# Two terms of a hand-written planner: how VectorE is shared with a cached-attention lane, and when TensorE takes a side step

## The chip, the cores and the metric

One Trainium2 chip, one NeuronCore. The metric is the device time of one launch in microseconds, as the median of several runs; for the kernel before it is 2890.09 us over three runs (2888.13 to 2892.71). The traces are of one further, profiled execution.

## The reference

Two decoder layers are computed for a prompt of 1,024 tokens and for 8 samples of 4 new tokens each, 1,056 rows of width 1,024 in all, with one set of weights, in float32. What matters here, in short:

```python
# layer 0: three dilated window attentions per head slot, mixed by their softmax weights
for g, (w, r) in enumerate(((128, 1), (512, 4), (2048, 16))):
    q, k = rope(rmsnorm(q)), rope(rmsnorm(k))
    prompt: o, lse = banded_attention(q, k, v)          # 128-wide bands, dilation r
    sample: s[b,t,h,j] = q . k_all[lb + t - r*j]        # j = 0..128, from the cache and the new rows
            o = softmax(s) @ v_all;  window buffers are shifted and returned
mix = sum_g softmax(lse)_g * o_g
# layer 1: S5 state space with GLU
# both layers: cross attention into 256 memory tokens, output projection, gated FFN with a width-3 convolution
```

`dilated_sample`, the sample's attention over its cached keys and values, is the part that the change names "the sample's cached attention". The rest of the two layers is the prompt's and the samples' projections, attentions, state space and FFN.

## The kernel before, in words

**Dense work.** Every projection runs on TensorE with activations and weights split in a high and a low part (three matmuls per product, `mm3`), in three column groups of 352 rows, into the four `pd` banks of PSUM. Weights come over the SyncE queue, ScalarE casts the high half (`whigh`) and VectorE subtracts the low half (`wlow`).

**Lanes.** All other work is written as Python generators, which sit in 14 queues, `self.lanes` (line 262 on). A generator issues some instructions and then yields what its next step needs: `yield x` means that the next step is TensorE's and reads tile `x`; `yield DVE, x` (or `ACT`, `POOL`) that it is another engine's; `yield WAIT` that it cannot go on yet. TensorE's steps of lanes are called side steps here; they write the four `pm` banks, and `pd` banks as well where the program only waits.

**The planner.** `Meter` (line 105 on) keeps a reckoned clock for every engine and a reckoned end for every written range. `note` (line 164) adds each instruction's cost by a formula: a matmul n/2400 + 0.0025 us, a VectorE operation 0.065 + 1.04 ns an element, 0.065 more with a scalar operand. `ready` (line 133) says when a step's inputs are there, with 0.2 us for another engine's result (0.06 for TensorE's own, 0.12 for VectorE's). These clocks only decide the order in which instructions are written down; on the chip each engine runs its own stream, and semaphores hold it where data is missing.

**The pump.** After every `mm3` of a dense product the kernel calls `pump` (line 329). It sets `now` to TensorE's reckoned clock + 0.1 us and calls `wtick` (line 390), which writes the casts and low halves of the next weights if ScalarE's or VectorE's clock is not past `now`. Then it goes through the lanes, by when their next step is due, lane 2 last, and takes up to four steps of each while `gate` (line 314) lies not past `now`; after one side step it leaves that lane. `gate` is the later of `due` (line 326, the inputs) and of the engine's clock, or for a side step of a free bank. Lane 2 is let through 0.6 us early. In `until` (line 360) the program writes no dense work; it sets `idle` and pumps until a condition holds, and a pump that moved nothing takes the step with the earliest gate.

**Lane 2** holds two kinds of generator. In layer 0 it is `swa` (line 1317), the samples' cached attention, one for each of 4 heads x 3 groups: on VectorE alone, it multiplies keys of the cache with the query (`tensor_tensor_reduce`, `M<-L,L` in the rows, and a read of the accumulator) and then adds scaled values (`scalar_tensor_tensor`, `L<-L,T,L`), with a `yield DVE` after each fifth product. Its first step needs the query, new key and value that `swa_prep` (line 1282, lane 1) has sent through DRAM (`scr`) with DMAs on GpSimd's queue; the cache comes in chunks over SyncE's queue. In layer 1 lane 2 holds `s5_out` (line 1821), whose steps are TensorE's.

**Around it.** `run` (line 2449) goes through the 12 pairs of head and group. Each turn begins with an `until` that lets at most 1, 2, 3 and 1 generators stand in lanes 0 to 3, then writes three dense projections (and on some turns one of the cross attention's queries) and appends `attn` (line 1079, lane 0), whose `scores` (line 1138) go to lanes 3 and 13, `swa_prep` and `swa`. The cross attention's `cross_p` (line 911) and `cross_s` (line 952) and the mixing of the groups, `combine_head` (line 1198), run in other lanes. After the last turn come `mem_kv(1)`, an `until` for the first mixed half and `swa_final(0)` (line 1405), the output projection `out_half` (line 1918), an `until` for the second half, and `finish` (line 746). In layer 1 the S5 chain is `s5_states` (line 1783, lane 0), `s5_out` (lane 2), `glu_in` and `s5_final`; `glu` (line 1896) begins with an `until` on them; `cross_gather` (line 1926) fetches the cross attention's result for the second `out_half`.

The step that ends a group of five products, and the lane's early pass, read:

```python
                if pi % 5 == 4:
                    yield DVE
...
            for _ in range(4):
                if not len(lane) or self.gate(lane) > now + 0.6 * (lane is self.lanes[2]):
                    break
```

All instructions are recorded through one helper, so the rows give line 216 (L216) throughout; they are told apart by tiles: `pd` dense, `pm` side steps, `L` the cached attention's ring, queries and sums (and other large tiles), `M`, `S` and `T` small work tiles, `A` and `B` large ones.

Of the kernel before, what the change touches and what calls it, by code (L numbers as in the profile page):

```python
# [248 lines left out]
class Kernel:  # L249
# [64 lines left out]
    def gate(self, lane):  # L314

        if lane.has(WAIT):
            return math.inf
        if lane.side():
            first = self.m.t[lane.gate[0]]
        else:  # L320
            first = self.m.bank_free("m", PM) if self.m.taken("m") < PM - 1 else math.inf
            if self.idle and self.m.taken("d") < PD - 1:
                first = min(first, self.m.bank_free("d", PD))
        return max(first, self.due(lane))

    def due(self, lane):
        return self.m.ready(lane.gate[lane.side():], lane.gate[0] if lane.side() else "tensor") if not lane.has(WAIT) else math.inf
# [1 line left out]
    def pump(self, force=False):  # L329
        now, moved = self.m.t["tensor"] + 0.1, False  # L330
        self.wtick(now)
        for lane in sorted((x for x in self.lanes if len(x)), key=lambda x: (x is self.lanes[2], self.due(x))):
            if len(lane) and lane.has(WAIT):
                lane.step()
                moved |= not lane.has(WAIT)
            for _ in range(4):
                if not len(lane) or self.gate(lane) > now + 0.6 * (lane is self.lanes[2]):
                    break
                side = lane.side()
                lane.step()  # L340
                moved = True
                if not side:
                    break
        if force and not moved:
            lanes = [x for x in self.lanes if len(x)]
            if lanes:
                min(lanes, key=lambda x: (self.gate(x), x in self.lanes[0:3:2], self.due(x))).step()
        if self.bulk and self.bulk_on and now > self.bulk_at:
            self.bulk_at = now + 24.0
            o, i = self.bulk.popleft()  # L350
            self.nc.sync.dma_start(out=o, in_=i)
# [1890 lines left out]
    def up_out(self, ht, ua, ub):  # L2242

        a, b = self.B(), self.B()
        yield from self.conv_sb(ht, ua, a)
        tail = self.conv_sb(NHT + ht, ub, b)
        next(tail)
        yield
        next(tail)
        gate = self.hidden(ht, a, b)  # L2250
        next(gate)
        yield
        for _ in tail:
            pass
        self.convs = ht + 1
        yield
        yield from gate
# [363 lines left out]
```

## Time and profile before

| | |
|---|---|
| median of three runs | 2890.09 us (2888.13 to 2892.71) |
| the profiled execution | 2884.84 us |
| its span, first to last instruction | 2883.1 us |
| mean granted TensorE clock | 0.976 |
| VectorE busy | 2047.9 us (71%) |
| ScalarE busy | 1216.7 us (42%) |
| GpSimd busy | 517.6 us (18%) |

A row of a timeline reads: start and length in microseconds, engine, line, operation, tile written <- tiles read, shapes, count, and in brackets how long the engine had been idle before and what released it. PE is TensorE's matmuls, PEld its weight loads, DVE VectorE, ACT ScalarE, POOL GpSimd. PEclk is the TensorE clock that was granted, as a share of full speed (2.4 GHz at 1.0, 1.2 GHz at 0.5).

### The profile page before, as it was taken

Reading aid. Unit: us, or ns where it says so; the run is one execution under the profiler, and the core shown is the slowest. Engines: PE = TensorE matmul, PEld = TensorE weight load, DVE = VectorE, ACT = ScalarE, POOL = GpSimd, SP = SyncE. Lnnn points to the kernel's source line nnn. Section 1 sums busy time; section 2 is a strip of 40 time slices with the busy share of each in tenths; the row PEclk is TensorE's granted clock in tenths of the full one; section 3 lists DMA queues with packets and bytes.
Section 4 is the critical chain, followed back from the end, with each engine's and each line's share of the span. In section 5 each row is a group of like instructions: output and inputs, shape, how many; then the busy total and the mean of one; then the engine's idle time right before and its main releaser. Section 6 shows DMA issues by size and latency. Waiting matters only on the chain. (4 is left out here: it accounts for less than half of the span.)

```text
span 2883.1 us, 50916 instructions
## 1 busy us (share of the span) xinstructions
PE 2713.7 (94%) x18896; PEld 2601.1 (90%) x18896; DVE 2047.9 (71%) x5918; ACT 1216.7 (42%) x3045; POOL 517.6 (18%) x773
## 2 busy tenths in 40 slices
PE   7999888899979999999999998988999999999999
PEld 5999877899969999999999898877999999999998
DVE  7466876788885787878859776645477877876444
ACT  6555545455541544444432124346254444443111
POOL 2111222313222500000102555310241000000000
PEclk8999999999989999999999999999999999999999
DMA  7235567667673423333464435943443333346421
GB/s 251 85 93 146 174 185 218 197 178 198 186 202 129 155 92 115 125 119 122 156 224 140 157 118 158 269 116 113 159 141 125 125 118 104 118 133 244 150 79 68
DMA packets 357315, 431.56 MB, mean 150 GB/s; under 512 B 30502, under 2 KB 310196, under 8 KB 355644
## 3 DMA queue, kind: packets, MB, share of 16 engines
q1 hardware_dynamic: 328604, 359.77, 39.3%
q0 software_dynamic: 28464, 68.55, 7.9%
q8 instruction: 149, 2.44, 0.4%
q14 instruction: 98, 0.80, 0.1%
HBM read 345.10 MB, written 172.37 MB: 179 GB/s over the span
## 5 line engine op out<-in xcount | busy, mean ns | idle before, releaser
L216 PE MATMUL pd<-A,B 128*128 128x352 f32 (+2 forms) x10992 | 1784.6, 316 | 48.8 <-DVE B L216 32.3
L216 PEld LDWEIGHTS pd<-A,B 128*128 128x128 f32 x10992 | 1641.1, 190 | 76.7 <-issue 37.3
L216 DVE TENSOR_TENSOR B<-B,B 128x512 fp32r<-128x512 f32 (+7 forms) x604 | 511.9, 856 | 220.5 <-ACT B L216 215.3
L216 ACT CAST B<-B 128x512 fp32r<-128x512 f32 (+4 forms) x430 | 313.9, 751 | 660.0 <-DVE B L216 337.3
L216 PE MATMUL pd<-L,B 128*128 128x264 f32 (+1 forms) x2976 | 445.5, 302 | 2.3 <-DVE B L216 1.8
L216 PEld LDWEIGHTS pd<-L,B 128*128 128x128 f32 x2976 | 415.8, 189 | 5.6 <-DVE B L216 2.7
L216 DVE TENSOR_TENSOR B<-pd,B 128x352 f32<-128x352 f32 x408 | 202.2, 518 | 191.0 <-PE pd L216 189.0
L216 ACT COPY B<-pm 128x512 f32<-128x512 f32 (+5 forms) x261 | 130.8, 509 | 198.3 <-PE pm L216 189.8
L216 PE MATMUL pd<-B,B 128*128 128x264 f32 (+2 forms) x1306 | 204.6, 306 | 7.2 <-DVE B L216 7.2
L216 DVE SCALAR_TENSOR_TENSOR B<-B,S,B 128x1023 f32<-128x1023 f32 (+1 forms) x152 | 194.1, 1277 | 0.0
L216 PEld LDWEIGHTS pd<-B,B 128*128 128x128 f32 x1306 | 181.8, 190 | 11.2 <-ACT L L216 7.1
L216 PE MATMUL pm<-const,B 128*128 128x128 f32 (+6 forms) x1119 | 159.8, 272 | 25.1 <-DMA B<-in_g_mix 7.5
L216 PEld LDWEIGHTS pm<-const,B 128*128 128x128 f32 (+4 forms) x1119 | 129.7, 147 | 44.7 <-issue 20.9
L216 ACT COPY S<-pm 128x256 f32<-128x256 f32 (+5 forms) x277 | 87.5, 348 | 160.0 <-PE pm L216 132.3
L216 ACT COPY B<-pd 128x352 f32<-128x352 f32 (+4 forms) x211 | 105.4, 542 | 101.8 <-PE pd L216 96.7
L216 ACT CAST A<-B 128x352 fp32r<-128x352 f32 (+3 forms) x148 | 97.0, 668 | 109.7 <-DVE B L216 45.5
L216 ACT ACTIVATE B<-B 128x352 f32<-128x352 f32 (+3 forms) x127 | 94.2, 750 | 50.7 <-DVE B L216 45.5
L216 DVE SCALAR_TENSOR_TENSOR L<-L,T,L 128x128 f32<-128x128 f32 x404 | 110.6, 349 | 0.9 <-DMA L<-in_cache_win_kv 0.9
L216 DVE CUSTOM_DVE_ANT_0 M<-L,L 128x128 f32<-128x128 f32 x384 | 88.6, 290 | 27.1 <-DMA L<-scr 12.9
L216 POOL DMA_DIRECT2D out_s_conv<-B x12 | 6.2, 513 | 553.3 <-ACT B L216 553.3
L216 PE MATMUL pm<-const,S 128*128 128x128 f32 (+3 forms) x464 | 80.6, 281 | 24.2 <-ACT S L216 16.7
L216 ACT ACTIVATE B<-B,S 128x1056 f32<-128x1056 f32 x76 | 96.7, 1273 | 2.3 <-DVE B L216 2.3
(230 smaller groups left out, 2669.8 us busy)
## 6 DMA issues: line engine op xcount, KB each, us to landing
B<-in_w_up SPq DMA_DIRECT2D x88, 512.0 KB, 5.1
hd<-B SPq DMA_DIRECT2D x44, 528.0 KB, 3.0
B<-hd SPq DMA_DIRECT2D x44, 528.0 KB, 4.1
B<-in_w_down SPq DMA_DIRECT2D x44, 512.0 KB, 3.6
B<-in_w_in_a SPq DMA_DIRECT2D x40, 512.0 KB, 5.0
B<-xsp SPq DMA_DIRECT2D x32, 528.0 KB, 6.6
L<-in_cache_win_kv SPq DMA_DIRECT2D x16, 1024.0 KB, 8.6
L<-in_cache_win_kv SPq DMA_DIRECT2D x64, 256.0 KB, 5.9
```

The lines of the kernel that those rows point to most:

```text
L216: return f(*args, **kw)
```

## The change

The gate of a side step is put 0.8 us after its inputs are reckoned to be there, except while the program waits in `until`. In the pump, lane 2 gives up to one step instead of four, and it is no longer let through 0.6 us early; what holds for lane 2 holds for both kinds of generator in it.

```diff
--- before.py
+++ after.py
@@ -321,7 +321,7 @@
             first = self.m.bank_free("m", PM) if self.m.taken("m") < PM - 1 else math.inf
             if self.idle and self.m.taken("d") < PD - 1:
                 first = min(first, self.m.bank_free("d", PD))
-        return max(first, self.due(lane))
+        return max(first, self.due(lane) + (0.0 if self.idle or lane.side() else 0.8))
 
     def due(self, lane):
         return self.m.ready(lane.gate[lane.side():], lane.gate[0] if lane.side() else "tensor") if not lane.has(WAIT) else math.inf
@@ -333,8 +333,8 @@
             if len(lane) and lane.has(WAIT):
                 lane.step()
                 moved |= not lane.has(WAIT)
-            for _ in range(4):
-                if not len(lane) or self.gate(lane) > now + 0.6 * (lane is self.lanes[2]):
+            for _ in range(1 if lane is self.lanes[2] else 4):
+                if not len(lane) or self.gate(lane) > now:
                     break
                 side = lane.side()
                 lane.step()
```

## Rows read from the trace of the kernel before

**Rows 1.** The page, part 1: TensorE's busy time, share of the span, instructions.

```profile
PE 2713.7 (94%) x18896; PEld 2601.1 (90%) x18896; DVE 2047.9 (71%) x5918; ACT 1216.7 (42%) x3045; POOL 517.6 (18%) x773
```

**Rows 2.** Windows by stage; columns: us, busy PE, PEld, DVE, ACT, POOL, PEclk, DMA, GB/s.

```profile
80.00:290.00 210.00, 204.72 (x1355) 197.92 (x1355) 126.45 (x610) 112.91 (x371) 27.15 (x47) 0.99 0.36 107
290.00:580.00 290.00, 253.95 (x1780) 234.30 (x1779) 214.12 (x1089) 147.46 (x470) 82.22 (x127) 0.96 0.64 193
580.00:780.00 200.00, 194.91 (x1297) 189.49 (x1296) 169.60 (x874) 113.14 (x376) 49.72 (x78) 0.99 0.64 180
780.00:900.00 120.00, 102.08 (x574) 91.97 (x573) 96.29 (x363) 44.64 (x116) 27.58 (x35) 0.91 0.71 211
```

**Rows 3.** TensorE's waits, 290 to 580 us; columns: total us, times, longest.

```profile
PE pm L216 <- ACT B L216: 18.3, 6, 7.8
PE pm L216 <- ACT S L216: 12.9, 10, 3.4
```

**Rows 4.** VectorE's timeline from 523.5 us; columns: start, length, what, [idle before <-releaser].

```profile
524.33 0.86 DVE L216 TENSOR_SCALAR L<-L,T 128x128 f32<-128x128 f32 x4
525.11 4.28 DVE L216 SCALAR_TENSOR_TENSOR L<-L,T,L 128x128 f32<-128x128 f32 x16
529.31 0.15 DVE L216 TENSOR_TENSOR T<-B 128x4 f32<-128x4 f32 x1
```

**Rows 5.** TensorE's timeline, 523 to 533 us.

```profile
530.65 1.11 PE L216 MATMUL pm<-const,B 128*128 128x128 f32 x4 [4.77 <-ACT B L216]
```

**Rows 6.** TensorE's timeline, 318 to 326 us.

```profile
321.68 0.71 PE L216 MATMUL pm<-const,S 128*128 128x128 f32 x2 [3.44 <-ACT S L216]
...
325.58 0.86 PE L216 MATMUL pm<-const,S 128*128 128x128 f32 x2 [2.70 <-ACT S L216]
```

**Rows 7.** VectorE's timeline at 377 us.

```profile
377.26 1.78 DVE L216 CUSTOM_DVE_ANT_0 M<-L,L 128x128 f32<-128x128 f32 x1 [6.93 <-POOL B L216]
```

**Rows 8.** TensorE's timeline, 375 to 386 us.

```profile
383.84 1.08 PE L216 MATMUL pm<-B,M 128*32 128x256 f32 x8 [7.83 <-ACT B L216]
```

**Rows 9.** VectorE's groups by shape, 290 to 580 us; columns: count, busy, mean, idle before.

```profile
L216 DVE CUSTOM_DVE_ANT_0 M<-L,L 128x128 f32<-128x128 f32 x160 | 39.6, 296 | 20.8 <-POOL B L216 6.9 <-DMA L<-scr 6.6 <-DMA xo<-M 6.0
...
L216 DVE DVE_READ_ACCUMULATOR2_ANT T<- 128x1 f32 x192 | 15.6, 81 | 0.0
```

**Rows 10.** Windows after one wait and in the second layer; columns as in rows 2.

```profile
528.04:534.87 6.83, 4.22 (x17) 4.09 (x18) 6.38 (x23) 4.10 (x14) 3.13 (x3) 0.50 1.11 347
1908.90:1945.60 36.70, 24.70 (x160) 18.25 (x160) 24.63 (x92) 21.76 (x57) 4.64 (x7) 0.81 0.37 123
1945.60:2040.40 94.80, 86.51 (x669) 74.73 (x668) 48.70 (x142) 54.98 (x155) 11.51 (x18) 1.00 0.40 125
```

**Rows 11.** Timeline of all engines, 815 to 832 us.

```profile
822.51 0.29 DVE L216 CUSTOM_DVE_ANT_0 M<-L,L 128x128 f32<-128x128 f32 x1 [4.54 <-DMA L<-scr]
...
825.91 5.06 PE L216 MATMUL pd<-B,A 128*128 128x512 f32 x11 [7.89 <-DVE B L216]
```

**Rows 12.** TensorE's timeline, 852 to 870 us.

```profile
856.78 1.40 PE L216 MATMUL pd<-A,B 128*128 128x352 f32 x7 [2.91 <-DVE B L216]
```

**Rows 13.** VectorE's timeline, 843 to 862 us.

```profile
844.18 8.22 DVE L216 SCALAR_TENSOR_TENSOR L<-L,T,L 128x128 f32<-128x128 f32 x31
...
854.03 3.56 DVE L216 TENSOR_TENSOR B<-B,B 128x768 fp32r<-128x768 f32 x2
```

**Rows 14.** ScalarE's timeline, 2040 to 2052 us.

```profile
2048.35 1.08 ACT L216 CAST A<-B 128x1056 fp32r<-128x1056 f32 x1 [0.74 <-DMA B<-xo]
```

**Rows 15.** TensorE's timeline, 2054 to 2071 us.

```profile
2068.93 1.12 PE L216 MATMUL pd<-A,B 128*128 128x352 f32 x6
```

**Rows 16.** VectorE's timeline at 867 us.

```profile
867.22 0.22 DVE L216 TENSOR_TENSOR L<-pm,L 128x32 fp32r<-128x32 f32 x1 [0.28 <-ACT L L216]
```

**Rows 17.** TensorE's timeline, 918 to 926 us.

```profile
922.93 1.12 PE L216 MATMUL pd<-L,B 128*128 128x352 f32 x6
```

**Rows 18.** TensorE's timeline, 230 to 240 us.

```profile
236.92 0.30 PE L216 MATMUL pm<-const,M 128*32 128x64 f32 x2 [2.50 <-ACT M L216]
```

## The prediction, made before the changed kernel was run

> **What bounds the kernel now.** I read the page's busy times first: TensorE is busy for 2713.7 of 2883.1 us [rows 1]. The diff adds and removes no instruction, it only lets the planner write the same ones down in another order, so all there is to win is the idle 169 us and what a lowered clock costs. The windows by stage show where that lies [rows 2]. In attention's middle, 290 to 580 us, TensorE is busy for 253.95 of 290.00 us: 36.1 us idle, at a granted clock of 0.96. The stages on either side, with the same loop, lose 5.3 of 210 and 5.1 of 200 us. The passage out of attention, 780 to 900, loses 17.9 of 120 us at 0.91. TensorE's waits in 290 to 580 come next [rows 3]: 18.3 us in 6 waits and 12.9 us in 10, together 31.2, end with a ScalarE result for a `pm` bank, which in this stage is a side step; none of the listed waits is one of the dense projection.
>
> The timelines show two ways in which such a wait comes about. **Burst:** at 524.33 VectorE runs 4 and then 16 products of the cached attention, four steps of the lane and 5.14 us, before it takes up the next head-combining step at 529.31 [rows 4]; TensorE stands for 4.77 us until 530.65 [rows 5]. Two waits of 3.44 and 2.70 us, close together, have the same form [rows 6]. **Block:** before a head's first product VectorE can sit blocked, on a DMA's landing or on GpSimd; at 377.26 it starts after 6.93 us [rows 7], and TensorE's longest wait of the stage, 7.83 us, ends at 383.84 [rows 8].
>
> **The change, part by part.** *Lane 2 on VectorE.* A pump comes after three matmuls of 352 columns, by the planner's own formula 0.447 us. The old rule fills VectorE until the planner's clock for it is past now + 0.6; at the next pump it is then still 0.15 us ahead. All other VectorE steps and the weights' low halves ask for a clock not ahead of now, so while the cached attention has steps they get in only after a longer pump (a side step on TensorE), although lane 2 is sorted last. The new rule asks the same of lane 2 as of the others and takes one step a pump. The planner also reckons a score product at 0.198 us; the rows give 39.6/160 + 0.081 = 0.33 us [rows 9], so four steps put VectorE 2.6 us later than planned, one step 0.65. At 530.65 one step ahead in place of four leaves 1.3 of the 5.14 us: 3.9 saved. Of the 3.44 and 2.70 I take half, 3.1, since five to ten products stood directly ahead there, not twenty. Sum -7.0. Bounds: 0, if the planner's clock lets four steps through in four pumps before the other step becomes ready, and -10.9, all three waits gone.
>
> *0.8 us on TensorE's side steps.* Without the four long waits (4.77, 3.44, 2.70, 7.83: 18.7 us) the 16 waits leave 12.5 us in 12, 1.04 each. While the side step is held back, dense matmuls run in its place, so each wait falls by up to 0.8: at most -9.6, at least 0 if the result is later by as much. I take -8, near the upper end, because the waits are about as long as the added time. The four long ones lose 0.8 each, -3.2; the 7.83 another 0.6, because the blocked product is also written down 0.6 later. With these the stage comes to -18.8.
>
> *Clock.* After the 4.77 us the granted clock is 0.50 for 6.83 us [rows 10], the lower of the two levels. At 0.96 the stage loses 0.04 x 290 = 11.6 us of clock, part of it while idle. Bounds 0 and -11.6; I take a third, -4, as the wait behind the block stays.
>
> *Passage out of attention.* The 7.89 us wait at 825.91 stands behind a blocked first product, 4.54 us, and two steps of the lane: 0.6 later and one step less (five products 0.21 apart, 1.1) give -1.7 [rows 11]. At 856.78 TensorE waits 2.91 us [rows 12] for low halves that come behind 31 products in a row, 8.22 us [rows 13]. With equal terms the low halves are asked first: -2.5 of 2.91. Sum -4.2, from 0 to -10.8.
>
> *The second layer's cross attention,* 1945.6 to 2040.4, has side steps among dense ones and 8.3 us idle [rows 10]; by the same 0.8 I take -6 (0 to -8.3). The quiet attention stages give a quarter of their 10.4 us: -2.5.
>
> *What it costs.* The 0.8 is a wait in the planner, not on the chip: nothing queues behind it on TensorE, and the one who waits is the reader of the side step's result. It doesn't hold where the program waits in `until`, because `idle` is set. At the start the normalisation's ones-matmul may come 0.8 to 1.6 us later: +1.6. In the second layer `s5_out` runs in lane 2: its TensorE steps lose the lead of 0.6 and gain 0.8; three in a row for the last quarter make +4.2 (from 0). Nothing covers it: 1908.9 to 1945.6 has no dense matmul and 12.0 us idle [rows 10], and the S5 chain ends it. The cross chain that follows gets about 10 us longer (some 13 held steps of 0.8), which I cost at nothing: the cast of its second gathered tile starts at 2048.35 [rows 14] and the dense matmuls that read it at 2068.93 [rows 15]; without that cover it costs its 10 us. The cached attention, now served last, is late next; I cost that at nothing too: its final result is written at 867.22 [rows 16], the residual projection that reads it begins at 922.93 [rows 17]. If those 55 us were used up, TensorE would stand there. SP and POOL queues get the same DMAs; fetches move with the products by a step or two, and no TensorE wait listed above ends with them.
>
> Sum: -18.8 - 4.0 - 4.2 - 6.0 - 2.5 + 1.6 + 4.2 = -29.7, say -30. The profiled execution took 2884.84 us (2883.1 span and 1.7 around it), which gives 2854.8; the three timed runs have a median of 2890.09, 0.18% above it, so the forecast is **2860**.
>
> **The rivals.** *A, nothing gained.* The lateness is one of blocks. One step a pump each 0.447 us is still more than VectorE can do (1.6 us a step), so a burst is only spread, the blocked first products stay, and the short waits turn up again one step later. For it: the two longest waits, 7.83 and 7.89, stand behind blocked products [rows 7, 8, 11]. Against it: the runs where nothing blocks [rows 4, 13]. The gain shrinks to the short waits' half, about -5 in attention and -4 in the second layer, against +5.8: -3, or 2887. The Trainium skill, page "TensorE: Matmul & The Clock Gate", section on the array's architectural detail, says that VectorE's and ScalarE's queues are strictly first in, first out; by that rule the blocked product still holds all behind it. The trace agrees: VectorE does nothing else in the 6.93 us [rows 7].
>
> *B, slower.* The held steps lengthen attention's chains until the `until` at the head of each loop turn has to wait. An `attn` has ten held TensorE steps and the `scores` behind it five: 12 us a turn. No such place shows today; the nearest row is a wait of 2.50 us at 236.92, among side steps with no dense one between [rows 18]. If the eight turns from 290 us on all end in one like it, they cost 20 us, the S5 and start terms 5.8, and some -14 stays: +12, 2902. It decides when a turn's chain lasts longer than two turns, some 120 us (twelve turns in about 730 us). Against it: in the crowded 290 to 580 the waits are scattered among dense matmuls, not gathered at turns.
>
> *C, more gained.* With VectorE no longer held by lane 2, the stage falls to its neighbours' idle, 2.5%: 36.1 to 7.3, and the clock with it (-8), the passage by 10 and the second layer by 8, no cost: -55, 2835.
>
> **How the numbers follow.** The forecast has 0.58, A 0.17, B 0.15, C 0.10. A measurement of this kernel tells 0.2%, 5.8 us, from no change. Forecast and C are faster, with a small part of A (0.03): 0.71. The rest of A is 0.14, B is 0.15. The forecast's own range by its bounds is 2840 to 2880; C's end and A lie beside it, so 2835 to 2895 leaves out most of B and a little beyond C, under 2 in 10.
>
> **What would show it.** Right: in 290 to 580 TensorE idle near 17 us, its waits on ScalarE near 13 in place of 31.2, hardly a run of products over ten on VectorE while others wait, the 2.91 us gone, a 6 to 7 us wait behind a blocked first product still there, the stretch without dense work before 1945 some 4 us longer. Wrong: idle there unchanged (A); stretches of over 3 us of side steps alone at the turns (B); or TensorE standing ahead of the residual projection for the cached attention's last tile.

## The result, and the profile after

Over four runs each, the changed kernel has a median of 2840.09 us (2835.74 to 2843.57) and the kernel before 2891.40 us: a ratio of 0.9824 with an interval of 0.9807 to 0.9841, or 51 us. The profiled execution took 2835.74 us with a span of 2833.6, at a mean granted clock of 0.983 in place of 0.976. It is the fastest of its four, which differ by 8 us among themselves, so a difference of a few microseconds in one stage of one trace is no finding here.

The page's busy times of the kernel after, to be set beside [rows 1]:

```profile
PE 2695.2 (95%) x18896; PEld 2594.1 (92%) x18896; DVE 2050.7 (72%) x5912; ACT 1216.4 (43%) x3045; POOL 524.1 (18%) x779
```

TensorE has the same 18896 matmuls. Its idle time fell from 169.4 to 138.4 us, and its busy time by 18.5 us with the same matmuls, at the higher clock. Six instructions moved from VectorE to GpSimd (5918 to 5912 and 773 to 779): some low halves go to whichever of the two the planner's clocks favour, so more changes than the order, to which the prediction had limited it. Windows cut at fixed times hold other work once the kernel is faster, so the first layer is cut by its work here: the attention loop from the second projection to the last (one window), and the passage from there to the first matmul of the output projection. Windows of the kernel before; columns as in rows 2:

```profile
76.90:788.40 711.50, 665.08 (x4505) 633.18 (x4505) 520.71 (x2610) 380.76 (x1248) 159.12 (x252) 0.98 0.57 166
...
788.40:843.00 54.60, 40.23 (x189) 31.33 (x188) 43.84 (x187) 28.38 (x61) 11.37 (x19) 0.84 0.84 235
```

The same two stretches of the kernel after, and below them the stage of [rows 2] with its old bounds:

```profile
76.50:759.90 683.40, 657.64 (x4506) 634.94 (x4505) 517.60 (x2591) 381.65 (x1249) 158.11 (x251) 0.99 0.59 171
...
759.90:798.60 38.70, 34.82 (x187) 28.17 (x186) 34.90 (x94) 25.79 (x52) 16.06 (x21) 0.96 0.81 247
...
290.00:580.00 290.00, 273.28 (x1922) 258.18 (x1923) 230.76 (x1145) 155.01 (x499) 80.11 (x124) 0.98 0.68 198
```

The matmul counts of the loop and of the passage show that it is the same work. The loop is 28.1 us shorter: 20.7 less idle (46.4 to 25.8) and 7.4 less busy. The passage is 15.9 us shorter: 10.5 less idle (14.4 to 3.9), and the rest is the clock, 0.84 to 0.96. Between 290 and 580 us TensorE is idle for 16.7 us in place of 36.1, but this window with fixed bounds holds 1922 matmuls now and held 1780 before.

TensorE's waits in that stage, after; columns as in rows 3:

```profile
PE pm L216 <- DMA B<-in_cache_mem_kv: 8.3, 3, 5.7
PE pm L216 <- ACT S L216: 4.8, 3, 2.7
PE pm L216 <- issue: 4.0, 2, 3.3
PE pm L216 <- ACT B L216: 2.3, 2, 2.1
```

The two ScalarE rows were 31.2 us in 16 waits [rows 3] and are 7.1 in 5. What ends last now is a DMA, the cross attention's cached keys and values, behind which side steps stand; its longest wait, 5.7 us, began 3 us before the window ("issue" is a wait for nothing that the profile shows).

The passage in TensorE's timeline, after:

```profile
793.90 1.22 PE L216 MATMUL pm<-B,B 128*128 128x128 f32 x4 [2.92 <-DVE T L216]
...
796.91 1.90 PE L216 MATMUL pd<-const,L 128*128 128x64 f32 x16
798.62 3.60 PE L216 MATMUL pd<-A,B 128*128 128x352 f32 x21
```

The end of the same passage before:

```profile
840.85 2.43 PE L216 MATMUL pd<-const,L 128*128 128x64 f32 x16
843.04 1.23 PE L216 MATMUL pd<-A,B 128*128 128x352 f32 x3
```

The 7.89 us of [rows 11] has no counterpart; the longest wait is now 2.92 us. The stretch without dense work that followed it before, from 830.97 [rows 11] to 843.04, is gone too: the `x16` transposes end a stretch with dense matmuls in it, and the output projection follows at once.

The end of the cached attention, in the timeline of VectorE and then of TensorE, after:

```profile
870.05 1.65 DVE L216 TENSOR_SCALAR L<-L,T 128x128 f32<-128x128 f32 x8
874.97 0.21 DVE L216 TENSOR_TENSOR L<-pm,L 128x32 fp32r<-128x32 f32 x1 [3.27 <-ACT L L216]
875.47 0.22 DVE L216 TENSOR_TENSOR L<-pm,L 128x32 fp32r<-128x32 f32 x1 [0.28 <-ACT L L216]
```

```profile
874.50 1.21 PE L216 MATMUL pd<-A,B 128*128 128x352 f32 x6
875.54 4.05 PE L216 MATMUL pd<-L,B 128*128 128x352 f32 x24
```

Before, the last tile was written at 867.22 and the residual projection came to it at 922.93 [rows 16, 17], 55 us later. Now it is written 8 us later, and TensorE comes 47 us earlier: nothing is to spare, though TensorE doesn't yet wait.

In the second layer, the windows of the S5 stretch and of what follows it up to the second FFN, first after, then (the second alone) before:

```profile
1853.50:1890.10 36.60, 24.60 (x159) 18.21 (x160) 24.64 (x92) 21.70 (x57) 4.63 (x7) 0.81 0.38 123
1890.10:2154.40 264.30, 251.82 (x1685) 236.91 (x1685) 159.14 (x360) 118.30 (x279) 67.58 (x76) 0.97 0.42 135
```

```profile
1945.60:2203.70 258.10, 247.70 (x1685) 232.55 (x1684) 160.67 (x362) 118.37 (x279) 64.98 (x74) 0.99 0.42 134
```

The S5 stretch is what it was, 36.6 us [rows 10]. The other is 6.2 us longer with the same 1685 matmuls, 4.1 of it at a lower clock.

**Where the 49.5 us of the span came from** (2883.1 to 2833.6): start -0.4, loop -28.1, passage -15.9, output projection up to the residual -3.0, from there to the S5 stretch -8.0, the S5 stretch -0.1, what follows it +6.0 (rounded parts).

### The profile page after: what moved, and what is told of

Its sections match the earlier page's. It is cut to its first block, busy times and chain, and to the rows that moved or that the text cites. A ratio compares the mean times of both kernels' runs of the same rounds, so it can differ in the third digit from the quotient of the medians.

```text
span 2833.6 us, 50973 instructions
## 1 busy us (share of the span) xinstructions
PE 2695.2 (95%) x18896; PEld 2594.1 (92%) x18896; DVE 2050.7 (72%) x5912; ACT 1216.4 (43%) x3045; POOL 524.1 (18%) x779
## 5 line engine op out<-in xcount | busy, mean ns | idle before, releaser
L216 PE MATMUL pm<-const,B 128*128 128x128 f32 (+5 forms) x1111 | 156.5, 271 | 27.1 <-DMA B<-in_cache_mem_kv 8.3
L216 ACT COPY S<-pm 128x256 f32<-128x256 f32 (+4 forms) x283 | 90.7, 347 | 164.2 <-PE pm L216 148.7
L216 ACT COPY B<-pd 128x264 f32<-128x264 f32 (+4 forms) x210 | 103.3, 545 | 82.6 <-PE pd L216 82.4
L216 DVE CUSTOM_DVE_ANT_0 M<-L,L 128x128 f32<-128x128 f32 x384 | 90.0, 289 | 19.2 <-DMA L<-scr 16.7
L216 POOL TENSOR_TENSOR A<-B,A 128x352 fp32r<-128x352 f32 (+2 forms) x77 | 82.0, 1092 | 81.9 <-ACT A L216 81.8
```

The source lines that it names most:

```text
L216: return f(*args, **kw)
```

## The experiments

"Loop", "passage" and "residual" are the stretches above (from the second projection, to the last matmul of the loop, to the output projection's first matmul, to the residual's), "rest" is all that follows, each read from the kernel's own trace in us; what is missing to the span lies ahead of the loop (76.0 to 81.7 us). A trace is one execution, so a stage of it scatters more than the ratio does (see E9). Ratios are to the kernel before on the same chip, with a 95% interval.

| kernel | lead | steps | wait | ratio | loop | passage | residual | rest |
|---|---|---|---|---|---|---|---|---|
| before | 0.6 | 4 | 0 | 1 | 711.5 | 54.6 | 79.9 | 1960.2 |
| after | 0 | 1 | 0.8 | 0.9824 (0.9807 to 0.9841) | 683.4 | 38.7 | 76.9 | 1958.1 |
| E1 | 0.6 | 4 | 0.8 | 0.9978 (0.9966 to 0.9990) | 707.8 | 51.8 | 77.4 | 1961.7 |
| E2 | 0 | 1 | 0 | 0.9899 (0.9883 to 0.9915) | 696.4 | 42.7 | 82.2 | 1959.0 |
| E3 | 0 | 4 | 0 | 0.9914 (0.9898 to 0.9930) | 697.6 | 38.6 | 86.1 | 1955.5 |
| E4 | 0.6 | 1 | 0 | 1.0069 (1.0052 to 1.0086) | 689.6 | 82.4 | 88.8 | 1958.0 |
| E5 | 0 | 1 | 0.4 | 0.9814 (0.9789 to 0.9839) | 681.3 | 38.1 | 79.9 | 1955.8 |
| E6 | 0 | 1 | 1.6 | 0.9933 (0.9907 to 0.9959) | 687.1 | 41.4 | 78.8 | 1976.3 |
| E7 | 0 | 4 | 0.8 | 0.9920 (0.9889 to 0.9951) | 692.6 | 43.5 | 79.9 | 1962.1 |
| E8 | 0 | 1 | 0.8, DMA reckoned later | 0.9893 (0.9861 to 0.9925) | 685.1 | 42.8 | 76.7 | 1969.0 |
| E9 | 0 | 1 | 0.8 in layer 0 | 0.9828 (0.9805 to 0.9851) | 689.8 | 36.1 | 78.4 | 1963.4 |
| E10 | 0 | 1 | 0.4 in layer 0 | 0.9810 (0.9794 to 0.9825) | 681.8 | 37.4 | 78.3 | 1961.5 |
| E11 | 0 | 1 | 0.6 | 0.9820 (0.9804 to 0.9837) | 682.8 | 36.0 | 76.1 | 1959.5 |
| E12 | -0.6 | 1 | 0.8 | 0.9960 (0.9944 to 0.9976) | 686.6 | 40.2 | 104.6 | 1963.6 |

### E1: the wait of 0.8 alone

```diff
-        return max(first, self.due(lane))
+        return max(first, self.due(lane) + (0.0 if self.idle or lane.side() else 0.8))
```

> Only the 0.8 us on TensorE's side steps; lane 2 keeps four steps and its lead of 0.6 us. My sum: the wait carries the larger half, 18 us of 30 by the forecast, some 25 of the 51 measured; 2865 us, ratio 0.991, the bursts of twenty products and the 2.9 us wait for low halves in the passage out of attention still there. Rival 'lane alone': nothing, ratio 1.00. Rival 'wait alone': the whole, 0.982. Rival 'luck of the order': any value from 0.98 to 1.01, not tied to the waits it should shorten.

Measured: 2880.63 us against 2885.85, 0.2% faster. Loop and passage are 3.7 and 2.8 us shorter. With lane 2 as before, the passage still has its long wait; VectorE's timeline and then TensorE's, of this kernel:

```profile
821.33 0.29 DVE L216 CUSTOM_DVE_ANT_0 M<-L,L 128x128 f32<-128x128 f32 x1 [5.07 <-DMA L<-scr]
```

```profile
829.13 0.86 PE L216 MATMUL pd<-const,S 128*128 128x128 f32 x2 [8.87 <-ACT S L216]
```

The first product is blocked for 5.07 us on the DMA of its gathered tile, as in [rows 11], and a wait of 8.87 us stands behind it. Only the first 1.1 us of that wait lie in the block; then VectorE works off 16 products, a low half and 5 more products. The wait of 0.8 us alone, which I thought the larger half of the forecast, is worth next to nothing.

### E2: lane 2's two edits, without the wait

```diff
-            for _ in range(4):
-                if not len(lane) or self.gate(lane) > now + 0.6 * (lane is self.lanes[2]):
+            for _ in range(1 if lane is self.lanes[2] else 4):
+                if not len(lane) or self.gate(lane) > now:
```

> Only lane 2: one step a pump and no lead; no 0.8 us. My sum: 2870 us, ratio 0.993, the passage out of attention (780 to 843 us) shorter by 10 us and more, the short waits of 1 us in 290 to 580 still there. Rival 'lane alone': 0.982. Rival 'wait alone': 1.00.

Measured: 2857.10 us, 1.0% faster. The loop is 15.1 us and the passage 11.9 us shorter. These edits are the larger part alone, but with the wait as well it is 0.9824: the wait, worth 0.2% by itself, is worth 0.75% here.

### E3: only the lead of 0.6 removed

```diff
-                if not len(lane) or self.gate(lane) > now + 0.6 * (lane is self.lanes[2]):
+                if not len(lane) or self.gate(lane) > now:
```

> Only the lead of 0.6 us is taken from lane 2; four steps a pump stay, no 0.8 us. My sum: the lead is what starved the low halves and the other lanes, so most of what the lane edit gives comes from here: 2873 us, 0.994. Rival 'the four steps matter': 1.00.

Measured: 2860.78 us, 0.86% faster: nearly all that E2 gains, the intervals overlap. The passage is 38.6 us, as after.

### E4: one step a pump, the lead kept

```diff
-            for _ in range(4):
+            for _ in range(1 if lane is self.lanes[2] else 4):
```

> Only one step a pump for lane 2; the lead of 0.6 us stays, no 0.8 us. My sum: little, 2887 us, 0.998 to 1.00, since a step of the lane is longer than a pump and the lead still keeps VectorE's clock ahead of the others. Rival 'the four steps matter': 0.993 or less, with no run of twenty products left in which another step is kept waiting.

Measured: 2904.16 us, 0.7% slower. The loop is 21.9 us shorter, and the passage 27.8 us longer, 82.4 in place of 54.6. But the loop of this kernel holds 71 matmuls less than that of the kernel before, which come in the passage and behind it; columns as in rows 2:

```profile
77.20:766.80 689.60, 654.80 (x4434) 624.92 (x4433) 494.54 (x2468) 369.33 (x1215) 149.56 (x240) 0.98 0.56 162
766.80:849.20 82.40, 47.35 (x216) 36.78 (x215) 59.37 (x239) 31.65 (x65) 19.31 (x26) 0.79 0.74 210
```

So the idle time tells more: 11.6 us less in the loop (34.8 for 46.4), 20.7 us more in the passage (35.1 for 14.4). ScalarE's timeline in the passage, then TensorE's, then SyncE's:

```profile
829.46 1.04 ACT L216 CAST A<-B 128x1024 fp32r<-128x1024 f32 x1 [14.45 <-DMA B<-xm]
830.41 0.40 ACT L216 ACTIVATE S<-S,T 128x128 f32<-128x128 f32 x1
```

```profile
830.95 1.18 PE L216 MATMUL pd<-const,S 128*128 128x128 f32 x3 [16.67 <-ACT S L216]
...
844.95 1.18 PE L216 MATMUL pd<-const,S 128*128 128x128 f32 x3 [5.67 <-ACT S L216]
```

```profile
824.57 0.34 SPq L216 DMA_DIRECT2D B<-xm  x1
```

The cast of a part of the mixed half comes to ScalarE before its gather (`xm`) has landed, holds ScalarE for 14.45 us, and the activation behind it is what TensorE waits for, 16.67 us. SyncE issues that gather only at 824.57, behind loads of the residual and of weights: 9.6 of the 14.45 us pass before the gather is on its way. The Trainium skill, page "TensorE: Matmul & The Clock Gate", section on the array's architectural detail, has ScalarE's queue strictly first in, first out; the trace agrees, since ScalarE does nothing in those 14.45 us. The three kernels with the lead have passages of 51.8 to 82.4 us, the eleven others 36.0 to 43.5: the lead is what made the passage long. Why one step with it makes it longer still wasn't followed further than these rows.

### E7: the wait without the lead, four steps

```diff
-            for _ in range(1 if lane is self.lanes[2] else 4):
+            for _ in range(4):
```

(against the kernel after)

> The changed kernel with four steps a pump for lane 2 instead of one (no lead, 0.8 us). Lead alone gave 0.9914, lead and one step 0.9899: one step adds 0.0015 without the wait. My theory now: 0.984, nearly the whole change. Rival 'one step is needed with the wait': 0.988 or more.

Measured: 2861.10 us, 0.8% faster: what E3 gives without the wait. So without the lead neither one step (E3 to E2) nor the wait (E3 to E7) does much alone, and both together bring it from 0.9914 to 0.9824. The 26.2 us between the spans of this kernel and of the kernel after are spread: 5.2 ahead of the loop, 9.2 in it, 4.8 in the passage, 3.0 up to the residual and 4.0 behind. One of TensorE's longer waits in the loop; timeline of all engines of this kernel:

```profile
456.11 0.29 DVE L216 CUSTOM_DVE_ANT_0 M<-L,L 128x128 f32<-128x128 f32 x1 [4.89 <-PE pm L216]
...
459.72 0.29 DVE L216 CUSTOM_DVE_ANT_0 M<-L 128x128 f32<-128x128 f32 x1
...
460.93 0.53 ACT L216 ACTIVATE T<-T 128x4 f32<-128x4 f32 x2 [1.23 <-DVE T L216]
...
461.36 0.80 ACT L216 COPY S<-pm 128x128 f32<-128x128 f32 x3
...
461.94 1.11 PE L216 MATMUL pm<-const,B 128*128 128x128 f32 x4 [4.30 <-ACT S L216]
```

Eighteen products run on VectorE from 456.11 to 460.01. ScalarE stands at the cached attention's own exponential, which needs the maximum after them, and the copies that TensorE's side step waits for stand behind that. A burst of 3.9 us isn't bridged by 0.8, and this one comes on top of a block, the 4.89 us that its first product waited. But four steps aren't what makes such bursts: the kernel after has them too (see the part on the prediction). Why one step and the wait pay only together is open; no run shows it wait by wait.

### E5, E6 and E11: the size of the wait

The kernel after with 0.4, 1.6 and 0.6:

```diff
-        return max(first, self.due(lane) + (0.0 if self.idle or lane.side() else 0.8))
+        return max(first, self.due(lane) + (0.0 if self.idle or lane.side() else 0.4))
```

> The changed kernel with 0.4 us in place of 0.8. The lane edit alone gave 0.9899 and the whole change 0.9824, so the wait is worth 0.0075 beside it. If it works by the size of the short waits, half the wait gives about half of that: 0.986, 2846 us against 2886. Rival 'luck of the order': no relation to the size; any value between 0.978 and 0.995 is as likely.

> The changed kernel with 1.6 us. The waits left on side steps in attention are few and not of this size, so a longer wait gives little more there, and every chain gets longer again: 0.982 to 0.987. Rival B of the prediction (chains reach the heads of the loop turns) would show here first: slower than the changed kernel by 10 us and more, with stretches of side steps alone at the turns. Rival 'luck': no relation.

> The changed kernel with 0.6 us, between two sizes that were measured alike. If the wait works by its size, it is like them: 0.981 to 0.983, the loop of attention (first turn's second projection to the last projection's end) near 682 us as with 0.4 (681.3) and 0.8 (683.4). If the loop's gain is luck of the order, it lies anywhere between 680 and 697 us.

Measured: 2830.91 us with 0.4, 2836.55 with 0.6, 2866.15 with 1.6. Between 0.4 and 0.8 the ratios, 0.9814, 0.9820 and 0.9824, can't be told apart, and the loops are 681 to 683 us in all three. Three sizes write three different orders, so the gain is no accident of one order of instructions. With 1.6 some 31 us of it are gone (0.9933 less 0.9824), the larger part in the rest, +18.2. It falls in the first FFN and the preparation of S5, 868.9 us after and 888.4 here. TensorE's waits from 1001 to 1888 us of E6, and from 985 to 1853 us of the kernel after:

```profile
PE pm L216 <- DVE S L216: 10.0, 7, 6.4
PE pd L216 <- DVE S L216: 4.6, 4, 1.6
```

```profile
PE pm L216 <- DVE S L216: 2.5, 4, 1.6
```

TensorE waits 12.1 us more for VectorE's small tiles. TensorE's timeline of E6 there:

```profile
1719.15 1.23 PE L216 MATMUL pd<-L,B 128*128 128x352 f32 x6 [0.64 <-DVE B L216]
...
1726.97 0.45 PE L216 MATMUL pm<-const,S 128*128 128x128 f32 x1 [6.37 <-DVE S L216]
...
1738.85 1.54 PE L216 MATMUL pd<-A,B 128*128 128x352 f32 x4
```

From 1720.38 to 1738.85 TensorE has side steps alone, one at a time between waits: a chain of held steps has become the longer road there. This is rival B's mechanism, at twice the size and in a place that I had not named.

### E8: the planner reckons GpSimd's DMAs to land later

```diff
-            self.dma[eng] = max(self.dma.get(eng, 0.0), self.t[eng] + 1.6) + n * out.ap[0][1] * 4 / 350e3
+            self.dma[eng] = max(self.dma.get(eng, 0.0), self.t[eng] + (4.0 if eng == "gpsimd" else 1.6)) + n * out.ap[0][1] * 4 / 350e3
```

(against the kernel after)

> The changed kernel, with the planner's time for a DMA on GpSimd's queue set 2.4 us longer (4.0 for 1.6), which is nearer to the 5.6 us that the trace shows for the 256 KB replies of the cached attention. If what is left of the loss in attention are blocks, VectorE's waits on the scr tiles (16.7 us in five) and TensorE's on the memory cache (8.3 us in three) go and the time falls by 5 to 10 us: 0.979. If they are covered by then: 0.982, no change. Rival: later issue of the first products moves the lane's end towards the residual projection: 0.984 and up.

Measured: 2854.71 us, 0.9893: slower than the change. VectorE has no wait on the `scr` tiles left from 60 to 870 us, but its score products in the loop still wait for 21.1 us, now for others; in the kernel after it is 19.2. So this run doesn't tell what the blocks cost TensorE. The loop is no shorter, 685.1 us; the rest is 10.9 us longer, and why wasn't traced.

### E9 and E10: the wait in the first layer alone

```diff
+        self.hold = 0.8
...
-        return max(first, self.due(lane) + (0.0 if self.idle or lane.side() else 0.8))
+        return max(first, self.due(lane) + (0.0 if self.idle or lane.side() else self.hold))
...
+        self.hold = 0.0
         self.lanes[0].append(self.s5_init())
```

(against the kernel after; E10 begins with 0.4)

> The changed kernel with the 0.8 us held only up to the second layer. The stages say that the wait makes the stretch from the S5 wait to the second FFN longer: 264.3 us against 258.1 before and 261.4 without it, where the prediction had a gain of 6. Theory: that stretch falls back to about 260 us and the time by 3 to 6 us, to 0.980. Rival 'luck of the order': the stretch stays where it is, 0.982 or more.

> The same with 0.4 us. If the wait is worth as much at 0.4 as at 0.8 (0.9814 and 0.9824 so far) and its cost lies in the second layer alone: 0.979 to 0.980, faster than both kernels of the case. Rival: 0.982.

Measured: 2837.79 and 2834.47 us. Both shorten the stretch after S5 from 264.3 to 261.6 us, but the medians can't be told from the kernel after, nor from E5. Nor does the stretch go by the wait: it is 260.8 us in E5 and E11, which hold the wait there, and 259.2 in E6 with 1.6. E9 also shows how far one trace may be trusted: up to the second layer it writes the same instructions as the kernel after, and yet its loop takes 689.8 us in place of 683.4, and its residual projection begins at 882.4 in place of 875.5. (The traced execution is the slowest of E9's four, and that of the kernel after the fastest of its four.)

### E12: lane 2 let through 0.6 late

```diff
-                if not len(lane) or self.gate(lane) > now:
+                if not len(lane) or self.gate(lane) > now + -0.6 * (lane is self.lanes[2]):
```

(against the kernel after)

> The changed kernel with lane 2 held back by 0.6 us more (its gate not past now - 0.6). If what counts is that lane 2 stands behind the others, it has that already: the loop stays near 683 us and the passage near 39, 0.982. If VectorE's own slack counts, there is a little more, 0.978. Rival: the lane's end now comes late for the residual projection, or VectorE stands idle: 0.986 and up, the loop longer.

Measured: 2878.33 us, 0.9960: most of the gain is gone, and 27.7 of the 42.7 us between the spans go in one place, the stretch up to the residual projection, 104.6 us in place of 76.9. VectorE's timeline there, then TensorE's:

```profile
887.03 9.53 DVE L216 SCALAR_TENSOR_TENSOR L<-L,T,L 128x128 f32<-128x128 f32 x36
...
913.71 0.22 DVE L216 TENSOR_TENSOR L<-pd,L 128x32 fp32r<-128x32 f32 x1 [0.28 <-ACT L L216]
```

```profile
904.83 0.24 PE L216 MATMUL pm<-const,M 8*128 8x8 f32 x1 [18.17 <-DVE T L216]
...
912.68 5.52 PE L216 MATMUL pd<-L,B 128*128 128x352 f32 x19
```

TensorE has nothing else left and stands for 18.17 us; the cached attention's last 36 products take 9.5 of them, and VectorE's steps behind them most of the rest. The cover that had shrunk from 55 us to none after the change is overdrawn here. So lane 2 can be too late as well as too early: 0.6 early is slower than 0 in each pair that was run (before and E3, E4 and E2, E1 and E7), and 0.6 late is slower too. Sizes between weren't run.

No kernel is shown faster than the change: E5, E10 and E11 have lower ratios, all inside its interval.

## Why the prediction was right, and where it was off

The sign and the main place were right; 2860 was 20 us too high, and the result lies near the lower end of the range, close to rival C.

- **Idle time in 290 to 580.** I forecast near 17 us; it is 16.7, a closer match than the working earned, since the window holds other work now. For the whole loop the terms were -18.8, -4 and -2.5, in sum -25.3, and the loop lost 28.1. But the split was wrong, and that the sum fits is in part luck. "Sum -7.0" for lane 2 and some -12 for the wait are, when each is tried alone, -15.1 (E2) and -3.7 us (E1) of loop. The terms were added as if they were independent; over the whole time they are not (0.9978 and 0.9899 alone, 0.9824 together), which the traces of before couldn't show.
- **"hardly a run of products over ten on VectorE while others wait"** came true only in its second half. Counted from VectorE's timelines, 290 to 580 us have 15 runs of over ten products with nothing but their accumulator reads between them before, the longest of 26, and 13 after, the longest of 42; E7 with four steps has 13, the longest of 40. Over the whole loop there are 31 before, 22 after, 21 in E3 and 27 in E7, both with four steps, and the longest are 37, 42, 42 and 40. So the bursts stayed, and one step a pump is not what makes them fewer: the working by "one step ahead in place of four", from which its 3.9 us came, is a step that failed, and the stage came out near the forecast without it. What changed is that TensorE no longer waits long behind them. One of them after, and TensorE's timeline beside it:

```profile
564.44 5.60 DVE L216 SCALAR_TENSOR_TENSOR L<-L,T,L 128x128 f32<-128x128 f32 x21
```

```profile
562.57 11.32 PE L216 MATMUL pd<-A,B 128*128 128x352 f32 x69
```

- **"four steps put VectorE 2.6 us later than planned"** was wrong too. My 0.33 us added two rows that overlap: score products follow each other every 0.21 us, so twenty are some 0.2 us later than the planner's 0.198 each. The 16 scaled values of [rows 4] took 4.28 us, 0.27 each, and the planner's formula gives 0.263. The planner's prices for lane 2 were right.
- **"a 6 to 7 us wait behind a blocked first product still there"** was wrong. Blocks remain, but no TensorE wait of more than 3 us in the stage ends with ScalarE any more. In VectorE's groups by shape, 290 to 580 us of the kernel after, the idle time ahead of the score products is 8.7 us in place of the 20.8 of [rows 9]:

```profile
L216 DVE CUSTOM_DVE_ANT_0 M<-L,L 128x128 f32<-128x128 f32 x160 | 40.6, 290 | 8.7 <-DMA L<-scr 6.1
```

  That, too, is the window. Over the whole loop, before and then after, it hardly fell, from 22.5 to 19.2 us. The blocks are still there, and TensorE waits less behind them:

```profile
L216 DVE CUSTOM_DVE_ANT_0 M<-L,L 128x128 f32<-128x128 f32 x352 | 81.5, 290 | 22.5 <-DMA L<-scr 8.3 <-POOL B L216 6.9 <-DMA xo<-M 6.0
```

```profile
L216 DVE CUSTOM_DVE_ANT_0 M<-L,L 128x128 f32<-128x128 f32 x352 | 82.9, 289 | 19.2 <-DMA L<-scr 16.7
```

- **Clock.** -4 forecast; the loop's busy time fell by 7.4 us for the same matmuls, and the passage's by 5.4.
- **Passage out of attention** is the term most mis-sized: -1.7 of the -4.2 up to the output projection, and -15.9 measured. I took off a few tenths from the wait in [rows 11] and left what stood behind it alone. E1, E3 and E4 show that the lead makes the whole stretch long: without it (E3) neither the 7.89 us nor the stretch of side steps behind it occurs. The other -2.5, for the low halves of [rows 12], came as -3.0, and the 2.91 us wait is gone.
- **Costs.** The start was to cost 1.6 us and cost nothing (76.9 to 76.5); `s5_out` was to cost 4.2 and cost nothing (36.7 to 36.6). The second contradicts the prediction's own premise: the stretch without dense matmuls is the `until` at the head of `glu`, and there the 0.8 doesn't hold. The S5 chain that ends the stretch didn't get longer.
- **Second layer's cross attention:** -6 forecast, +6 measured, so the term has the wrong sign. E9 and E10, without the wait in this layer, have 2.7 us less, and so has E2, which never had it, but E5, E11 and E6 have 3.5 to 5.1 us less with it. So the wait gains nothing there, and what the +6 comes from is open: the order, or the scatter of one trace.
- **Cover of the cached attention:** I cost it at nothing and named 55 us as what hides it. That held, with nothing left over, and E12 shows the price beyond it: 104.6 us up to the residual in place of 76.9.
- **Rivals.** A fell: the idle time is not unchanged. B fell for 0.8: stretches of over 3 us without a dense matmul occur seven times in the loop before and three times after. It came true in part at 1.6 (E6). C, that VectorE was held by lane 2 and the stage falls to its neighbours, is the nearest in time, and the passage shortened by more than its 10 us, but the stage kept 16.7 us of idle time where C has 7.3; its "no cost" was right for the start and S5 and wrong behind S5.

In the sum, the passage gave 14 us more than forecast, the loop 3, the avoided costs 6 and the unforecast stretch from the residual to S5 8 (of the size of the scatter that E9 shows), and the second layer took 12 back: about the 20 us by which I missed.

## What to carry to other kernels

In a hand-ordered program, be wary of giving a background lane a lead over work that TensorE's next side step depends on: here its early pass cost most at the hand-over between stages, not only where it runs. Terms of such a planner need not add up: here two that brought almost nothing one by one, with the lead gone, brought half of the gain together, so undo each alone before crediting it. Count a pattern that you hold guilty before and after: here the bursts were still there when the long waits behind them were gone. And when a lane is served last, look at what reads its final tile: the cover that makes the change free is spent by the change's own gain.

## What the runs showed of the hardware that was not expected

- One blocked instruction on ScalarE cost more than any on VectorE: 14.45 us on one gather in E4, with TensorE standing 16.67 us. Of it 9.6 us passed before a third engine's queue, SyncE's, issued the gather.
- The gathers of the cached attention's queries and new keys and values, `L<-scr`, 256 KB each on GpSimd's queue, land 5.6 us after issue in the median of the changed kernel's 36 (4.7 before), where the planner reckons 1.6 us and the bytes. Correcting that in the planner made the kernel slower (E8).
- Score products follow each other every 0.21 us when nothing is between them, though one is recorded as 0.28 to 0.29 and its read of the accumulator as 0.08. Eighteen took 3.9 us (E7), so a row's length here is not the price of one more instruction.
- The granted clock of the passage went from 0.84 to 0.96 when its idle time went from 14.4 to 3.9 us. That returned 5.4 us by itself, about half of what the idle time gave.
